# Storing the second-to-last row tile of an RMSNorm-matmul kernel by column chunk

## Chip, cores, metric

The kernel runs on 1 core of one Trainium2 chip. The metric is the device time in microseconds (us) of one execution. "Span" is the time from the first to the last instruction in a profile; the timed run of the same execution is 1.8 us longer in the kernel before.

## The reference, cut to what matters

```python
# x: (8, 1024, 768) f32, gamma: ones(768), w_qkv: (768, 2304) f32
rms = np.sqrt(np.mean(x ** 2, axis=-1, keepdims=True) + eps)
x_norm = x / rms * gamma
return np.matmul(x_norm, w_qkv).astype(np.float32)
```

The kernel takes x as 8192 rows, that is 64 row tiles of 128, and makes 2304 columns for each: four chunks of 512 columns and one of 256.

## The kernel before

The weights are converted to bf16 once (with gamma in them) and stay in SBUF. For each row tile x is loaded, cast, transposed by DMA, and multiplied; the factor 1/rms is applied when PSUM is evicted. VectorE and ScalarE take the evictions in turn. A tile's output has three parts: columns 0 to 1023, 1024 to 2047, and 2048 to 2303.

```python
# cut; the comments are added here
PARTS = [(0, 1024), (1024, 1024), (2048, N - 2048)]
...
outp = ctx.enter_context(tc.tile_pool(name="outp", bufs=7))
...
def store(t, h, n0, nl):
    p0 = PARTS[h][0]
    nc.sync.dma_start(out=of[t * P:(t + 1) * P, n0:n0 + nl], in_=OUT[t, h][:, n0 - p0:n0 - p0 + nl])
...
def evac_at(time, t, n0, eng, gap):
    at(time, evac, t, n0, eng)
    h = part(n0)
    nl = min(NT, N - n0)
    left[t, h] = left.get((t, h), PARTS[h][1]) - nl
    if t == MT - 1:                                   # last tile: a store for each chunk
        at(time + gap - 0.5, store, t, h, n0, nl)
    elif left[t, h] == 0:                             # others: a store for each part
        at(time + gap, store, t, h, *PARTS[h])
```

`at` only puts operations in an order; the times in it are the author's plan. All loads, transposes and stores are issued by SyncE, in that order.

Of the kernel before, what the change touches and what calls it, by code (L numbers as in the profile page):

```python
# [89 lines left out]
def kernel(  # L90
# [21 lines left out]
    MT = M // P  # L112
# [119 lines left out]
    def part(n0):  # L232
        return max(i for i, (p0, _) in enumerate(PARTS) if p0 <= n0)
# [21 lines left out]
    def at(time, fn, *args):  # L255
        plan.append((time, len(plan), fn, args))
# [8 lines left out]
    def evac_at(time, t, n0, eng, gap):  # L265
        at(time, evac, t, n0, eng)
        h = part(n0)
        nl = min(NT, N - n0)
        left[t, h] = left.get((t, h), PARTS[h][1]) - nl
        if t == MT - 1:  # L270
            at(time + gap - 0.5, store, t, h, n0, nl)
        elif left[t, h] == 0:
            at(time + gap, store, t, h, *PARTS[h])
# [13 lines left out]
    for time, op, *args in HEAD_PLAN:  # L287
        if op == "evac":

            evac_at(time, *args, gap=max(1.0, LOADS[-1][0] + 0.1 - time))  # L290
        elif op[-1] in "AB":
            at(time, tr_half if op[:2] == "tr" else cp_half, args[0], op[-1], *args[1:])
        else:
            if op == "mm":
                args[2] = [int(k) for k in args[2]]
            at(time, ops[op], *args)
# [4 lines left out]
    for t in range(HEAD, MT):  # L301

        ahead = 6.0 if t < HEAD + 5 else 0.0
        if ("x", t) not in {q[1:] for q in LOADS}:
            at(now - 15 - ahead, load_x, t)
        at(now - 8.5 - ahead, cast, t)
        at(now - 7.5 - ahead, xbar, t)
        at(now - 5, stat, t)
        at(now - 3, recip, t)
        for n0 in range(0, N, NT):  # L310
            at(now, mm, t, n0, range(KO))
            now += min(NT, N - n0) * US
            flip ^= 1
            evac_at(now + 0.2, t, n0, "DVE" if flip else "ACT", gap=1.2)
# [38 lines left out]
```

## Time and profile before

| | before |
|---|---|
| time, 3 runs | 389.31 us median (389.13 to 389.34) |
| span of the profiled run | 387.4 us |
| TensorE busy | 381.7 us, 99% |
| main matmuls in the chain that ended last | 94% of the span, without a break from 20.1 to 383.4 us |
| last store: issue, landing | 383.95 us, 2.0 us later |
| from the last issue to the end of the span | 3.44 us |

Some words for the end of the program. A store has "landed" when its completion semaphore has reached its full count, so that a waiting engine may go on. The DMAs use eight such semaphores in turn, the "lanes". At the close of the program SyncE makes five "closing checks", each of which waits for two semaphores, then a "drain", and then all engines meet in a barrier. "The step" is a gap of 0.39 us between the starts of two of these checks that no wait explains. A "record" is one line of SyncE's list in the trace.

Where this document gives times to three digits, they are taken from the instruction and DMA records of the trace.

### The profile page before, as it was taken

Reading aid. Unit: us, or ns where it says so; the run is one execution under the profiler, and the core shown is the slowest. Engines: PE = TensorE matmul, PEld = TensorE weight load, DVE = VectorE, ACT = ScalarE, POOL = GpSimd, SP = SyncE. Lnnn points to the kernel's source line nnn. Section 1 sums busy time; section 2 is a strip of 40 time slices with the busy share of each in tenths; the row PEclk is TensorE's granted clock in tenths of the full one; section 3 lists DMA queues with packets and bytes.
Section 4 is the critical chain, followed back from the end, with each engine's and each line's share of the span. In section 5 each row is a group of like instructions: output and inputs, shape, how many; then the busy total and the mean of one; then the engine's idle time right before and its main releaser. Section 6 shows DMA issues by size and latency. Waiting matters only on the chain.

```text
span 387.4 us, 5550 instructions
## 1 busy us (share of the span) xinstructions
PE 381.7 (99%) x1994; PEld 195.0 (50%) x1994; DVE 153.7 (40%) x309; ACT 181.2 (47%) x362; POOL 7.5 (2%) x15
## 2 busy tenths in 40 slices
PE   8999999999999999999999999999999999999995
PEld 7444654554554554554554554554554554554552
DVE  3565524434333344333344333344333343333331
ACT  5762444443544443544444544444444544444531
POOL 1312000000000000000000000000000000000000
PEclk9999999999999999999999999999999999999999
DMA  8999999999999999999999999999999999999975
GB/s 291 387 270 396 331 357 351 370 361 330 294 299 310 312 293 311 300 305 309 305 299 308 301 306 306 305 302 313 282 319 313 291 309 289 318 310 294 292 251 190
DMA packets 89223, 119.91 MB, mean 310 GB/s; under 512 B 52326, under 2 KB 61292, under 8 KB 89196
## 3 DMA queue, kind: packets, MB, share of 16 engines
q1 hardware_dynamic: 89184, 119.56, 101.1%
q8 instruction: 15, 0.25, 0.3%
q14 instruction: 12, 0.10, 0.1%
q10 hardware_dynamic: 12, 0.00, 0.0%
HBM read 32.25 MB, written 75.50 MB: 278 GB/s over the span
## 4 chain that ended last, share of the span: by engine, by line
PE 94%; DMA 4%; SPq 0%; DVE 0%; ACT 0%; issue 0%
PE pm L229 94%; DMA w_f<-in_w_qkv_dram 4%; SPq L153 0%; DVE w_b L164 0%; ACT ot L245 0%; SPq L158 0%
## 5 line engine op out<-in xcount | busy, mean ns | idle before, releaser
L229 PE MATMUL pm<-w_b,xT 128*128 128x512 bf16 (+1 forms) x1920 | 373.9, 358 | 0.6 <-DVE w_b L164 0.6
L229 PEld LDWEIGHTS <-xT 128*128 128x128 bf16 x1920 | 187.7, 98 | 186.1 <-issue 0.8
L243 DVE TENSOR_SCALAR ot<-pm,rstd 128x512 f32<-128x512 f32 (+1 forms) x165 | 113.6, 693 | 201.0 <-PE pm L229 200.7
L245 ACT ACTIVATE ot<-pm,rstd 128x512 f32<-128x512 f32 (+1 forms) x155 | 100.2, 648 | 190.6 <-PE pm L229 143.9
L183 ACT ACTIVATE sq<-x_t 128x768 bf16<-128x768 f32 x64 | 53.4, 834 | 2.0 <-DMA x_t<-in_x_dram 2.0
L172 DVE CAST xb<-x_t 128x768 bf16<-128x768 f32 x61 | 33.2, 544 | 18.2 <-DMA x_t<-in_x_dram 18.2
L185 ACT ACTIVATE rms<-ssq,eps_sb 128x1 f32<-128x1 f32 x64 | 18.9, 295 | 2.1
L183 ACT ACTIVATION_READ_ACCUMULATOR sq<-x_t 128x1 f32 x64 | 12.3, 192 | 0.0
L190 DVE RECIPROCAL rstd<-rms 128x1 f32<-128x1 f32 x64 | 9.8, 153 | 3.2 <-ACT rms L185 3.2
L166 ACT ACTIVATE w_b<-w_f,g_sb 128x512 bf16<-128x512 f32 (+1 forms) x9 | 5.8, 669 | 6.0 <-DMA w_f<-in_w_qkv_dram 6.0
L168 POOL TENSOR_SCALAR w_b<-w_f,g_sb 128x512 bf16<-128x512 f32 (+1 forms) x9 | 6.8, 765 | 24.3 <-DMA w_f<-in_w_qkv_dram 16.2
L164 DVE TENSOR_SCALAR w_b<-w_f,g_sb 128x512 bf16<-128x512 f32 (+1 forms) x12 | 5.2, 449 | 3.9 <-DMA w_f<-in_w_qkv_dram 3.9
L278 PE MATMUL pm<-warm 128*128 128x128 bf16 x49 | 5.4, 301 | 1.0 <-DVE eps_sb L137 1.0
L278 PEld LDWEIGHTS <-warm 128*128 128x128 bf16 x49 | 4.9, 142 | 1.0 <-DVE eps_sb L137 1.0
L210 PE MATMUL pm<-ident_f,x_t 128*128 128x128 f32 x18 | 2.5, 278 | 0.1
L210 PEld LDWEIGHTS pm<-ident_f,x_t 128*128 128x128 f32 x18 | 1.9, 141 | 0.5 <-DMA x_t<-in_x_dram 0.3
L172 DVE CAST xT<-pm 128x512 bf16<-128x512 f32 (+1 forms) x3 | 1.8, 592 | 0.5 <-PE pm L210 0.5
L140 ACT ACT_TABLE_LOAD x1 | 1.3, 1283 | 1.3 <-PEq L334 1.3
L174 ACT CAST xT<-pm 128x256 bf16<-128x256 f32 (+1 forms) x3 | 1.2, 445 | 0.3 <-PE pm L210 0.2
L174 ACT COPY xT<-pm 128x768 bf16<-128x768 bf16 x1 | 0.8, 799 | 0.3 <-PE pm L196 0.3
L261 DVE COPY g_sb<-pm 128x6 f32<-128x6 f32 x1 | 0.2, 165 | 1.8 <-PE pm L260 1.8
L196 PEld LDWEIGHTS <-xb 128*128 128x128 bf16 x6 | 0.4, 98 | 0.2
(13 smaller groups left out, 2.4 us busy)
## 6 DMA issues: line engine op xcount, KB each, us to landing
out_dram<-ot SPq DMA_DIRECT2D x126, 512.0 KB, 4.0
x_t<-in_x_dram SPq DMA_DIRECT2D x64, 384.0 KB, 4.3
out_dram<-ot SPq DMA_DIRECT2D x64, 128.0 KB, 3.3
w_f<-in_w_qkv_dram SPq DMA_DIRECT2D x7, 768.0 KB, 7.7
w_f<-in_w_qkv_dram SPq DMA_DIRECT2D x4, 256.0 KB, 5.9
out_dram<-ot SPq DMA_DIRECT2D x4, 256.0 KB, 2.0
xT<-xb SPq DMA_TRANSPOSE x60, 4.5
w_f<-in_w_qkv_dram SPq DMA_DIRECT2D x1, 512.0 KB, 4.2
```

The source lines that it names most:

```text
L164: nc.vector.tensor_scalar(out=o, in0=i, scalar1=g, scalar2=None, op0=mult)
L166: nc.scalar.activation(out=o, in_=i, func=AF.Copy, scale=g, bias=0.0)
L168: nc.gpsimd.tensor_scalar(out=o, in0=i, scalar1=g, scalar2=1.0, op0=mult, op1=mult)
L172: nc.vector.tensor_copy(out=out, in_=in_)
L183: nc.scalar.activation(out=sq, in_=X[t], func=AF.Square, accum_out=ssq)
L185: nc.scalar.activation(out=rms, in_=ssq, func=AF.Sqrt, scale=inv_k, bias=eps_sb)
L190: nc.vector.reciprocal(out=r, in_=RS[t])
L210: nc.tensor.transpose(out=PT[t, h][:, ko - k0, :], in_=X[t][:, ko * P:(ko + 1) * P], identity=ident_f)
L229: nc.tensor.matmul(out=PM[t, n0][:, :nl], lhsT=XT[t][:, ko, :], rhs=w_b[:, ko, n0:n0 + nl], start=(b == 1), stop=(b == KO))
L243: nc.vector.tensor_scalar(out=o, in0=pm[:, :nl], scalar1=RS[t], scalar2=None, op0=mult)
L245: nc.scalar.activation(out=o, in_=pm[:, :nl], func=AF.Copy, scale=RS[t], bias=0.0)
L278: nc.tensor.matmul(out=wps, lhsT=warm, rhs=warm, start=True, stop=True)
```

## The change

Since the last tile is already stored chunk by chunk, so that its data leaves as early as it can, the same is done for the tile before it. The intent is to have fewer bytes under way when the last stores begin.

```diff
-        if t == MT - 1:
+        if t >= MT - 2:
             at(time + gap - 0.5, store, t, h, n0, nl)
```

For this tile, stores of 512, 512 and 128 KB become four of 256 KB and one of 128 KB.

## The prediction

> **What bounds the kernel now.** I read the page first, then the chain of waits in order of time, and then, because the change touches only the second-to-last of 64 row tiles, the last 15 us of the trace. The page:
>
> ```profile
> PE 381.7 (99%) x1994; PEld 195.0 (50%) x1994; DVE 153.7 (40%) x309; ACT 181.2 (47%) x362; POOL 7.5 (2%) x15
> PE 94%; DMA 4%; SPq 0%; DVE 0%; ACT 0%; issue 0%
> L229 PE MATMUL pm<-w_b,xT 128*128 128x512 bf16 (+1 forms) x1920 | 373.9, 358 | 0.6 <-DVE w_b L164 0.6
> ```
>
> TensorE is busy for 99% of the span, the chain that ended last is 94% main matmuls, and those 1920 recorded matmuls waited 0.6 us in all. The engine is never held up by an output buffer or a store. The chain of waits in order of time ends like this:
>
> ```profile
> 20.12 363.25 PE pm L229 x1872
> 383.38 0.02 issue
> 383.40 0.47 ACT ot L245
> ```
>
> From 20.12 to 383.37 us it is one unbroken run of matmuls. Only what follows 383.4 us is not matmul: the last eviction (to 383.87), the last store and the closing of the program (to 387.4). So a change of stores can alter the time in two ways only: it disturbs the matmuls, or it moves something in the last 4 us.
>
> **The tail, before.** The timeline of ScalarE, VectorE and the store queue, asked in short windows (start, duration):
>
> ```profile
> 374.32 0.69 ACT L245 ACTIVATE ot<-pm,rstd 128x512 f32<-128x512 f32 x1 [0.97 <-PE pm L229]
> 375.04 0.33 SPq L249 DMA_DIRECT2D out_dram<-ot  x1
> 376.91 0.69 ACT L245 ACTIVATE ot<-pm,rstd 128x512 f32<-128x512 f32 x1 [1.90 <-PE pm L229]
> 377.63 0.33 SPq L249 DMA_DIRECT2D out_dram<-ot  x1
> 378.08 0.35 SPq L249 DMA_DIRECT2D out_dram<-ot  x1
> 383.40 0.47 ACT L245 ACTIVATE ot<-pm,rstd 128x256 f32<-128x256 f32 x1 [1.26 <-PE pm L229]
> 383.95 0.38 SPq L249 DMA_DIRECT2D out_dram<-ot  x1
> ```
>
> The three issues at 375.04, 377.63 and 378.08 are the present stores of the tile in question; each follows the eviction of the last chunk in its part by about 0.03 us (374.32 + 0.69 = 375.01). The issue at 383.95 is the last store of the last tile. The DMA engines in half-microsecond stretches (after the stretch: the engines' busy times and counts, then granted clock, DMA share, GB/s):
>
> ```profile
> 375.00:375.50 0.50, 0.50 (x4) 0.27 (x3) 0.00 (x0) 0.01 (x1) 0.00 (x0) 1.00 0.00 0
> 380.00:380.50 0.50, 0.50 (x4) 0.25 (x3) 0.34 (x1) 0.00 (x0) 0.00 (x0) 1.00 0.51 184
> 382.50:383.00 0.50, 0.50 (x6) 0.41 (x5) 0.25 (x1) 0.00 (x0) 0.00 (x0) 1.00 0.03 8
> 384.50:385.00 0.50, 0.00 (x0) 0.00 (x0) 0.00 (x0) 0.00 (x0) 0.00 (x0) 1.00 1.02 385
> 386.00:386.50 0.50, 0.00 (x0) 0.00 (x0) 0.00 (x0) 0.00 (x0) 0.00 (x0) 1.00 0.00 0
> ```
>
> There are holes in the transfers around 375, around 380.2 and again just before 383. Nothing of the second-to-last tile is still queued when the last stores start. After the last issue, the closing wait on SyncE and the landing times in this stretch are:
>
> ```profile
> L348 SPq EVENT_SEMAPHORE  x1: 1562/1562/1562, 384.4 to 384.4; - x1
> out_dram<-ot SPq DMA_DIRECT2D x4, 256.0 KB, 2.0
> ```
>
> So the end is: eviction done 383.87, issue 383.95, all landed 384.39 + 1.56 = 385.95 (2.0 us after the issue), a row of further semaphore checks and a barrier among the engines to 387.4, 1.45 us. The timed run of this profile was 389.19 us, 1.8 us above its span.
>
> **What the Trainium skill says.** "DMA: Bandwidth & Descriptors", section "Anatomy of one DMA", puts a fixed cost of about 2.0 us on a DMA, mostly the receipt of the last byte, plus bytes over 436 GB/s; that fit is for DMAs issued by GpSimd. The trace agrees in kind, with less: a 256 KB store lands in 2.0 us where the formula gives 2.6, a 512 KB store in 2.6 where it gives 3.2. The slope is the same 0.6 us for 256 KB. The fixed part therefore is a latency, which lies beside matmuls for every store except the last. The same page, "Rules for kernel authors", advises 1 MiB or more per DMA for bandwidth; splitting goes against that, but in the tail the 256 KB stores already move at a DMA share of 1.0 with some 385 GB/s, and half the stretches have room. "Perfetto Trace Analysis", section "Per-instruction lifecycle", says that the record of a DMA instruction leaves out the movement of the data; the trace agrees: 0.33 us of issue against 2.0 us to landing. I therefore count the 0.33 us as SyncE's cost and take the movement from the stretches.
>
> **The change part by part.** For the second-to-last tile, whose evictions end at 373.78, 375.01, 376.37, 377.60 and 378.05 (starts plus durations of the timeline), the order of the built program shows that three stores (512, 512, 128 KB) become five (four of 256 KB, one of 128). PE is unchanged; VectorE and ScalarE have the same work in the same order. Only SyncE's list is different.
>
> Removed: the two stores of 512 KB issued at 375.04 and 377.63. Added: four of 256 KB which I expect at 373.81, 375.04, 376.40 and 377.63, by the same 0.03 us after the eviction; the store of 128 KB stays at 378.08. Bytes are equal. SyncE pays 2 more issues of 0.33 us and 2 more semaphore checks with gaps, about 2 x 0.43 = 0.86 us (0.43 is the distance between back-to-back issues, 383.53 to 383.95). All of it falls between 373.8 and 376.8, where the queue has only waits: on the path, 0. The data: 256 KB take 0.65 us at 400 GB/s, and arrive every 1.3 us, so the first half of each part is gone before the second is evicted. The tile's last byte lands perhaps 0.3 us earlier than now (its last two transfers carry 384 KB in place of 640 KB). Nobody waits for it: the last tile's five stores are released by its own evictions, and the final 256 + 128 KB begin after a hole at 382.5 to 383.0. Gain from it: 0.
>
> One by-product remains. Completion semaphores rotate over eight lanes, and two more stores shift the last five by two lanes. In the built program the closing checks on SyncE each take two lanes in a fixed order. Before, the very first check holds the lane of the last store, so four more checks and a drain come after the landing (records at 386.00, 386.07, 386.14, 386.53, then 386.62). After the change the first check holds the store before the last, the second one the last store. So one check slips under the wait: about 0.07 us less. The step from 386.14 to 386.53 has 0.36 us of idleness that no wait explains; the end of SyncE's list also moves, so if this comes from its position there it may be hidden as well. Sum: 0.07 certain enough, up to 0.43 if both, so 389.31 - 0.1 = 389.2 us.
>
> **The rivals.** (1) A new wait takes the place of none: a store has to wait until the DMA eight earlier in the lanes has landed. With ten stores at the end, the last store waits for the second store of the changed tile, issued at about 375.04, landed by 377.1, needed at 383.9: 6.8 us to spare. The tightest others are the last tile's first stores, which wait for DMAs issued before 372.4 and landed by some 375, over 4 us before their turn. If I misread this, one store would be late by a microsecond: 390.3. Nothing speaks for it.
> (2) SyncE becomes the bound at the end: two issues push all later ones by 0.86 us, giving 390.2. Against it: between 378.44 and 379.58 the queue is idle, and each later store starts 0.03 us after its eviction.
> (3) The tail gains a microsecond, because the large stores held back the last tile: 388.3. Against it: all four 256 KB stores of the last tile land in 2.0 us already, the first too, and only the last landing counts.
> (4) The finer stores disturb the matmuls through memory traffic. Evictions follow at 1.29 to 1.30 us (six matmuls) at 368.5 to 376.9, whether the DMA share is 1.0 or 0. So 0.
>
> **Range and chances.** The three runs before lie within 389.13 to 389.34. A rebuilt program and another chip may move all by 0.1%, 0.4 us, which is more than any effect that I found. Point 389.2; range 388.7 to 389.6. A change of 2% is 7.8 us, more than the whole 4 us outside the matmuls, so within 2% at 0.99, the rest split evenly.
>
> **What would show it.** In the profile after: PE still at 99% with the chain's run of matmuls ending near 383.4; store issues near 373.8, 375.0, 376.4, 377.6, 378.1, and then the same five as before; 2.0 us to landing; the 1562 ns check gone or shorter, the wait for the last store now in the second check, and a span of 387.0 to 387.4. Wrong would be: the last issue later than 0.1 us after the last eviction, DMA busy at 383, a wait at the closing checks past 386.0, or a matmul run that is longer by over 0.3 us.

## The result

The changed kernel took 389.13 us (median of 6 runs, 388.87 to 389.33) against 389.32 us (6 runs, 389.08 to 389.57) before. The ratio is 0.9995, with a 95% interval of 0.9982 to 1.0008: the same. A ratio here is the mean time of one kernel's fast runs over that of the other's of the same rounds, so it is not quite the ratio of the medians.

The page of the changed kernel, the lines that answer to those of before:

```profile
PE 381.7 (99%) x1994; PEld 194.7 (50%) x1994; DVE 153.9 (40%) x309; ACT 181.2 (47%) x362; POOL 7.5 (2%) x15
PE 94%; DMA 4%; POOL 0%; SPq 0%; ACT 0%; issue 0%
L229 PE MATMUL pm<-w_b,xT 128*128 128x512 bf16 (+1 forms) x1920 | 374.1, 358 | 0.5 <-DVE w_b L164 0.4
```

TensorE has the same 381.7 us, the chain is again 94% matmuls, and they waited 0.5 us in all. The end of the chain in order of time:

```profile
17.94 365.63 PE pm L229 x1883
383.56 0.03 issue
383.59 0.47 ACT ot L245
```

The run of matmuls ends at 383.56 in place of 383.37 us. Its length counts from another point at the head (17.94 or 20.12 us), which comes and goes between executions of the changed kernel: a second profile of the changed kernel begins it at 20.04 and ends it at 383.29. This is noise of the start, about 0.2 us either way. The store queue in the timeline, four of the tile's issues and then the last issue of all:

```profile
373.99 0.33 SPq L249 DMA_DIRECT2D out_dram<-ot  x1
375.22 0.33 SPq L249 DMA_DIRECT2D out_dram<-ot  x1
376.58 0.33 SPq L249 DMA_DIRECT2D out_dram<-ot  x1
377.81 0.33 SPq L249 DMA_DIRECT2D out_dram<-ot  x1
...
384.15 0.37 SPq L249 DMA_DIRECT2D out_dram<-ot  x1
```

With 0.19 us taken off for the later matmuls these are the predicted 373.8, 375.0, 376.4 and 377.6. The last eviction ended at 384.06 and its store was issued at 384.15: the store queue is not late. The DMA engines by stretch (the last two columns are their busy share and GB/s):

```profile
380.00:380.50 0.50, 0.50 (x4) 0.22 (x3) 0.15 (x1) 0.00 (x0) 0.00 (x0) 1.00 0.00 0
382.60:383.10 0.50, 0.50 (x6) 0.35 (x5) 0.17 (x1) 0.00 (x0) 0.00 (x0) 1.00 0.12 41
384.50:385.00 0.50, 0.00 (x0) 0.00 (x0) 0.00 (x0) 0.00 (x0) 0.00 (x0) 1.00 0.90 336
```

The hole near 380 has become wider, so the tile's bytes do leave earlier: by the DMA records nothing moves from 379.86 to 380.60, before from 380.28 to 380.41 only. The hole before the last stores was there already and has moved with the matmuls (382.78 to 383.18, before 382.59 to 383.00; this is why the second stretch shown begins 0.1 us later than that of the prediction, which would have 0.30). The first two closing checks of SyncE (duration in ns, then start):

```profile
L348 SPq EVENT_SEMAPHORE  x1: 28/28/28, 385.8 to 385.8; - x1
L348 SPq EVENT_SEMAPHORE  x1: 28/28/28, 386.3 to 386.3; - x1
```

The record of 1562 ns is gone; the check that follows the last landing is now the second. In the kernel before, the step lay between the fourth and the fifth check:

```profile
L348 SPq EVENT_SEMAPHORE  x1: 28/28/28, 386.1 to 386.1; - x1
L348 SPq EVENT_SEMAPHORE  x1: 28/28/28, 386.5 to 386.5; - x1
```

In the changed kernel no two of the checks after the landing lie so far apart (0.07 us each). From the last issue to the end of the span there are 3.19 us in place of 3.44, in the second profile 3.07. So the tail is 0.25 to 0.37 us shorter. This small gain is what the experiments had to explain: do the earlier bytes make it, or only the two stores more in SyncE's list, which move the closing checks?

### The profile page after: what moved, and what is told of

It reads as the page before. It is cut to its first block, busy times and chain, and to the rows that moved or that the text cites. A ratio compares the mean times of both kernels' runs of the same rounds, so it can differ in the third digit from the quotient of the medians.

```text
span 387.3 us, 5554 instructions
## 1 busy us (share of the span) xinstructions
PE 381.7 (99%) x1994; PEld 194.7 (50%) x1994; DVE 153.9 (40%) x309; ACT 181.2 (47%) x362; POOL 7.5 (2%) x15
## 4 chain that ended last, share of the span: by engine, by line
PE 94%; DMA 4%; POOL 0%; SPq 0%; ACT 0%; issue 0%
PE pm L229 94%; DMA w_f<-in_w_qkv_dram 3%; DMA x_t<-in_x_dram 1%; POOL w_b L168 0%; ACT ot L245 0%; SPq L158 0%; SPq L153 0%
```

## The experiments

The theory: the tile's stores lie beside the matmuls and are worth nothing, and what little is gained comes from having two stores more in SyncE's list before the closing. Three groups follow: what the closing does, what the tile's stores can cost, and what is the same in other tiles. Each edit is against the kernel before.

### The kernel before, profiled again (no edit)

> The kernel before, unchanged, profiled a second time. In its first profile the closing of the program has a step of 0.39 us between the starts of the fourth and the fifth semaphore check (386.14 to 386.53) that no wait explains; in the changed kernel's profile it is gone. Theory fixed step: it belongs to the program and comes again, 0.35 to 0.40 us, between the same two checks. Rival chance: it was a single event of that execution, and the fifth check now follows the fourth by about 0.07 us. Both: last matmul run ends within 0.3 us of 383.4, the last store lands 2.0 us after its issue.

One run, 389.23 us. The step came again: fourth check at 386.195, fifth at 386.583, 0.388 us apart, of which 0.360 us no record fills. From the last issue to the end 3.43 us. So it belongs to the program.

### The same shift without touching the tile

```diff
-        if t == MT - 1:
+        if t in (30, MT - 1):
```

> Tile 30 is stored in five stores in place of the second-to-last tile, which keeps its three. Same number of stores, same shift of completion lanes and the same length of SyncE's list as in the changed kernel, but the tail's stores are as before. Theory by-product: whatever the changed kernel gains at the end comes from the shift alone, so from the last issue to the end of the span there are 3.2 us here as in the changed kernel (before: 3.44), with no step of 0.36 us in the closing checks. Rival finer stores: the gain came from the tile's own stores, and the closing takes 3.44 us here. Total in both cases within 0.3 us of 389.2.

389.07 us against 389.52 of before on the same chip, ratio 0.9986 (0.9971 to 1.0001). From the last issue to the end 3.035 us, with no step in the checks. The second of them waits for the last landing, and the drain follows the fifth at 386.46.

```profile
L348 SPq EVENT_SEMAPHORE  x5: 28/28/28, 385.8 to 386.4; - x5
```

The second-to-last tile has its three old stores here, and the tail is as short as in the changed kernel, or shorter. The finer stores of that tile are not what shortens it.

### One store more

```diff
+        elif left[t, h] == 0 and h == 0 and t in (30,):
+            at(time + gap, store, t, h, 0, 512)
+            at(time + gap, store, t, h, 512, 512)
         elif left[t, h] == 0:
```

> Tail as in the kernel before; one 512 KB store of tile 30 cut in two, so one store more in all, the last store in completion lane 3 (the first closing check still waits for it), SyncE's list two instructions longer. For the unexplained step of 0.36 us three theories. Place in the list: the step sits at one fixed place of SyncE's instruction list, so it moves to the third closing check, and from the landing of the last store to the closing drain it takes some 0.67 us as before. Branch: it comes five instructions after the branch into the closing block, so it is at the fifth check again, also 0.67 us. Waiting in execution: it follows a check that waits for its second semaphore while executing, as in the kernel before (record of 1.56 us); here the last store is the first semaphore of the first check, so no step, and 0.31 us from landing to drain. Total within 0.3 us of 389.3.

One run, 389.39 us. The closing checks of this kernel (its closing line is L351), the first four:

```profile
L351 SPq EVENT_SEMAPHORE  x1: 28/28/28, 386.1 to 386.1; - x1
L351 SPq EVENT_SEMAPHORE  x1: 28/28/28, 386.2 to 386.2; - x1
L351 SPq EVENT_SEMAPHORE  x1: 27/27/27, 386.6 to 386.6; - x1
L351 SPq EVENT_SEMAPHORE  x1: 28/28/28, 386.7 to 386.7; - x1
```

The step is now between the second and the third check (386.213 to 386.601), two checks earlier, as the list is two instructions longer. From landing to drain 0.68 us. The branch theory (fifth check) and the theory of the wait in execution (no step) fall; the theory of place stands. The odd record of 1562 ns also has its rule: it appears where the last store's semaphore is the second of a check's two in the built program, and the record is 28 ns where it is the first, as here.

### Three stores more

The edit is the same with `t in (20, 25, 30)`.

> Tail as in the kernel before; three 512 KB stores in mid-kernel cut in two. The last store goes to completion lane 5, so the third closing check waits for it, and SyncE's list is six instructions longer. The unexplained step followed the place in SyncE's list so far (the fifth check before, the third with one store more, none seen with two). Theory place: here the place holds the issue of the last store itself, so the step of 0.36 us delays that issue: 0.45 to 0.55 us after the end of the last eviction in place of 0.08, and nothing hides it; from the last eviction to the end of the span 3.6 us (before 3.5). Rival: the step is a matter of the closing block alone; the issue follows the eviction by 0.08 us and no step appears. Total near 389.4 against 389.1.

One run, 389.43 us. The last eviction and the last issue in the timeline:

```profile
383.56 0.47 ACT L245 ACTIVATE ot<-pm,rstd 128x256 f32<-128x256 f32 x1 [1.26 <-PE pm L229]
384.45 0.33 SPq L249 DMA_DIRECT2D out_dram<-ot  x1
```

The eviction ends at 384.03 and the issue follows 0.43 us later; in all kernels of this tail without that step it follows by about 0.1 us. So the step can be moved onto the last store itself, and from the end of the eviction to the end of the span there are 3.61 us, as expected. The records show a regular place: SyncE's records 80, 208, 336, 464 and 592, counted from one, so 128 apart, have an idle time of 0.34 to 0.46 us before them in all fourteen traces, where adjacent records without a wait have some 0.05 us. The exception is a record that waits for other reasons as well, as record 592 of the changed kernel does (1.24 us), where the step cannot be told apart from the wait.

The traces also hold a hint of what happens there. The profile lists a DMA queue called "instruction", and from 376 us to the end the changed kernel has one packet of 8 KB on it:

```profile
q14 instruction: 1, 0.01, 0.2%
```

By the DMA records it begins at 385.70, 1.18 us after record 591 ended. In the other traces too an 8 KB packet follows 1.0 to 1.5 us after the end of record 591, wherever that lies between 381 and 390 us. In the kernel with chunks in all tiles record 591 ends at 281.5 us, the packet follows 2.6 us later, and there is none in the last 20 us of the span. So SyncE most likely fetches instructions at these places. Where the step can be seen it is over before the packet begins, so it is not a wait for this packet; what it consists of stays open.

### Five stores more, twice

The edit is the same with `t in (20, 25, 30, 35, 40)`.

> Tail as in the kernel before; five 512 KB stores of tiles 20 to 40 cut in two, which puts the last store in completion lane 7, so that the fifth and last closing check waits for it and the other four lie under its landing. Theory lanes: from landing to the closing drain about 0.1 us, where the kernel before has 0.67 and the changed kernel 0.27 or a little more; from the last issue to the end of the span 2.85 to 3.0 us (before 3.44, changed 3.2). Rival no effect of the lanes: 0.3 us or more from landing to drain. Total 388.8, that is 0.5 us less than before, which three rounds can hardly tell from the noise of 0.2 us; the trace decides.

> The kernel of split5 again, with more rounds, beside the changed kernel on the same chip. Theory: from the last issue to the end of the span 2.8 us again (before 3.44, changed 3.19), total 0.5 to 0.6 us under the kernel before, 388.7 to 389.0, ratio 0.9985. Rival noise: the same total as before within 0.2 us.

388.94 us against 389.52, ratio 0.9984 (0.9968 to 1.0001), and on another chip 388.84 against 389.50, ratio 0.9983 (0.9969 to 0.9998). The last issue and some closing checks of the first of the two:

```profile
384.09 0.38 SPq L249 DMA_DIRECT2D out_dram<-ot  x1
```

```profile
L351 SPq EVENT_SEMAPHORE  x1: 28/28/28, 384.5 to 384.5; - x1
...
L351 SPq EVENT_SEMAPHORE  x1: 28/28/28, 386.1 to 386.1; - x1
```

The first check is done at 384.5 and the last, which waits for the last store, begins at 386.06; the drain follows at 386.13. From the last issue to the end 2.79 us in both profiles, a little less than the expected 2.85 to 3.0. That is 0.64 us less than before and 0.28 to 0.40 less than in the changed kernel, without a change in the tail's own stores. This is the fastest kernel, though at 0.17% still "the same".

### The changed kernel again (no edit)

> The changed kernel again, with more rounds. Theory by-product: from the last issue to the end of the span 3.03 to 3.2 us, no step in the closing checks, total 0.2 to 0.4 us under the kernel before, ratio 0.9990 to 0.9995. Rival finer stores matter: 1 us or more less. Rival noise: ratio 1.0000 with both signs among the rounds.

389.06 us against 389.50, ratio 0.9987 (0.9971 to 1.0002). From the last issue to the end 3.07 us, no step. The medians lie 0.44 us apart, a little more than expected, but the interval still includes 1, so by the clock alone a gain is not shown; this trace shows 0.37 us, the first one 0.25.

### The tile in 36 stores

```diff
-        if t == MT - 1:
-            at(time + gap - 0.5, store, t, h, n0, nl)
+        if t >= MT - 2:
+            step = 64 if t == MT - 2 else nl
+            for c in range(n0, n0 + nl, step):
+                at(time + gap - 0.5, store, t, h, c, step)
```

> The second-to-last tile in 36 stores of 64 columns in place of 5. Theory issue cost: SyncE is a queue that needs 0.43 to 0.45 us for one store with its check; 36 of them from 373.8 us take until 389.5, and the five of the last tile follow, so the last issue comes at 391.3 in place of 383.95 and the total is 7.0 to 7.5 us longer, 396.5, slower by 1.8 to 1.9%, with the matmul run ending at 383.4 as before. Rival transfers: the small rows make the DMA engines the bound, so that landings take far over 2 us and the total is longer still. Rival hidden anyway: no change.

398.66 us, ratio 1.0234 (1.0218 to 1.0251): slower. The last eviction, which ends the chain of matmuls, and the last issue:

```profile
383.43 0.47 ACT ot L245
```

```profile
393.02 0.52 SPq L249 DMA_DIRECT2D out_dram<-ot  x1
```

The matmuls end as ever, and the store queue works on for 9 us. The mechanism is the expected one, issue cost on SyncE; its size was put too low. In this queue a small store takes 0.475 us, not 0.43 to 0.45, and one step (record 592) falls into it as well. The small stores land in 1.5 us (median), so the DMA engines are not the bound, and the rival of slow transfers falls. For the five larger stores that come last within 2 us, landing took up to 2.7 us.

### The tile in 18 stores

The same edit with `step = 128`.

> The second-to-last tile in 18 stores of 128 columns. Theory issue cost, with the 0.48 us for one small store that the run with 36 stores showed: 18 x 0.48 = 8.6 us from 373.8 end at 382.4, the last tile's stores catch up at 0.43 us each, and the last issue comes at 384.0 to 384.3, at most 0.3 us late; the lane shift (last store in the second closing check) gives 0.3 us back, so 389.2 to 389.5 in total. So 15 stores more cost nothing, 33 more cost 9 us. Rival proportional cost: each store added costs the same, 9.2 us / 33 x 15 = 4.2 us.

390.19 us against 389.46, ratio 1.0019 (1.0000 to 1.0038), some 0.7 us longer, where 389.2 to 389.5 was expected. The last issue is at 384.55 us, 0.67 us after the end of its eviction at 383.87, and I had expected at most 0.3. In the records the last tile's stores catch up at 0.47 to 0.50 us each rather than 0.43, and record 592, with 0.36 us of idleness before it, falls among the small stores before them. Back to back, the last stores land in up to 2.6 us. Still, 15 stores more for the tile cost 0.7 us and 33 more cost 9: cost in proportion (4.2 us) is refuted. Up to about this number there is room in the queue.

### The tile's three stores held back to the end

```diff
         if t == MT - 1:
+            if n0 + nl == N:
+                for k, part_ in enumerate(PARTS):
+                    at(time + gap - 0.6, store, t - 1, k, *part_)
             at(time + gap - 0.5, store, t, h, n0, nl)
-        elif left[t, h] == 0:
+        elif left[t, h] == 0 and t != MT - 2:
```

> The three stores of the second-to-last tile are held back until just before the last store: the same bytes and as many stores as before, but now in front of the last store. Theory: a transfer of this tile costs only where it stands ahead of the last store in the DMA queues. Three issues of 0.43 us put the last issue 1.3 us later, and 256 + 512 + 512 + 128 + 128 KB from 384.3 at 400 GB/s end at 388.3, so the last landing is near 388.7 in place of 385.95 and the total 2.5 to 3 us longer, 391.8 to 392.3. Rival, bandwidth of the tail does not matter: 1.3 us longer by the issues alone, 390.6.

391.96 us against 389.46, ratio 1.0064 (1.0047 to 1.0081), 2.5 us longer. The DMA engines by stretch and the issues:

```profile
385.00:386.00 1.00, 0.00 (x0) 0.00 (x0) 0.00 (x0) 0.00 (x0) 0.00 (x0) 1.00 1.01 406
386.00:387.00 1.00, 0.00 (x0) 0.00 (x0) 0.00 (x0) 0.00 (x0) 0.00 (x0) 1.00 1.01 401
```

```profile
384.81 0.97 SPq L249 DMA_DIRECT2D out_dram<-ot  x1
385.88 1.13 SPq L249 DMA_DIRECT2D out_dram<-ot  x1
```

Here the engines move the 1536 KB without a break from 384.28 to 388.47, and the first closing check ends at 388.85, where 388.7 was expected for the landing. The last two issues take 0.97 and 1.13 us in place of some 0.35, and the last comes some 2 us late; why is not settled. Since the engines never pause, the row of bytes sets the end and not the late issue. This shows what the change could have been good for: bytes of this tile cost time where they stand in front of the last store. In the kernel before they do not.

### The last tile in three stores

```diff
-        if t == MT - 1:
+        if t == MT:
```

> The last tile too is stored in three stores in place of five. Theory: what column chunks are worth they are worth in the last tile alone. The 512 KB of its second part start after the eviction at 383.5, in place of 256 KB, so the last landing is 256 KB / 400 GB/s = 0.65 us later; two stores less put the last store in completion lane 0, third closing check, which gives 0.14 us back, and the step of 0.36 us in the list moves past the checks or not. Total 0.1 to 0.7 us longer than before, 389.6 to 390.1. Rival: the fixed time to landing hides the size and nothing changes.

389.63 us against 389.46, ratio 1.0003 (0.9987 to 1.0018). The time to landing of the last two stores:

```profile
DMA to landing us min/median/max: 2.6/2.6/2.6
```

The last landing is 0.6 us later, as estimated. From the last issue to the end 3.72 us, only 0.28 more than before: the last store is waited for in the third check and the step has moved past the checks, so that from landing to drain there are 0.20 us in place of 0.67, and the step gives 0.16 us of this back in the barrier that follows. So chunks are worth 0.6 us at the last landing, in the last tile. The clock alone does not tell the two kernels apart.

### Chunks in all tiles

```diff
-        if t == MT - 1:
+        if t >= HEAD:
```

> All tiles from the seventh on are stored by column chunk, five stores in place of three, 114 issues more in all. Theory: stores lie beside the matmuls all along, SyncE needs 5 x 0.43 + 1.3 (transpose) + 0.4 (load) = 3.9 us of a tile's 5.8 us, so no wait appears and the total is within 0.4 us of 389.2. Rival traffic: finer stores disturb matmuls or delay the loads and transposes behind them in SyncE's list, and the matmul run gets holes: over 390.

390.06 us (389.32 to 390.57) against 389.46, ratio 1.0017 (0.9998 to 1.0036), which is not clear of noise. The expectation of 389.2 within 0.4 was missed by the median. The one profiled execution was the fastest of the four, and its matmuls waited 0.6 us in all and ended at 383.62, so it shows no cost. The other executions had spans of 387.9 to 388.5 and no profile: whether something was lost there, and where, stays open. About half of the 0.6 us by which the median exceeds that of the kernel before lies outside the span: in all four executions the timed run is 2.1 us longer than the span, before 1.8. The interval's upper end bounds it at 0.4%.

## Why the prediction was right

**The bound.** The step "one unbroken run of matmuls" held. The matmuls of the main line waited 0.6 us before and 0.5 us after in all, and the run ends between 383.3 and 383.7 us in the kernels whose ends were read, even where the store queue is 9 us behind.

**The issues.** The 0.86 us of extra SyncE work lay in idle time, as the issue times show; the last store still follows its eviction by 0.09 us. The price of 0.43 us for an issue was right for single stores. In a row it was 0.475 us, so the term of the sum was low by a tenth. This had no weight in the changed kernel and gave wrong sizes in the two runs with many stores.

**The data.** "Gain from it: 0" was right. Its side estimate, that the tile's last byte lands 0.3 us earlier, was low: 380.20 in place of 380.63, and 0.62 us earlier when the later matmuls are taken off. The "hole around 380.2" that the prediction read was in truth only 0.13 us long before the change, but the last tile's first store was not held back by it: its bytes move 0.83 us after its issue, as those of the next one do. The hole grew, and nobody waited for what was gained there. The held-back run shows that it would have counted if those bytes had stood before the last store.

**The by-product.** The prediction gave 0.07 us for the check that slips under the wait, and up to 0.43 us if the unexplained step depended on its place in the list. It does: one, three and five stores more moved it as its place says. From the start of the second check to the drain there were 0.62 us before and 0.27 us after, so 0.35 us of the 0.43 came true inside the checks. In the first profile of the changed kernel the last store took 0.12 us longer to be seen as landed (2.17 us from issue to the second check, 2.05 in the kernel before), which leaves 0.23 of the 0.25 us seen there; the rest lies behind the drain. In one detail the prediction misread the list: the fourth and fifth check hold one lane each, beside a semaphore that is none of the eight. The checks that its argument needs do hold two.

**The signs.** Two of the marks that I had named for "wrong" were met by the letter. The matmul run was longer by over 0.3 us (365.63 in place of 363.25), but only because it counts from another point at the head; its end moved by 0.19 us. And the second check began at 386.3, past 386.0. It was no new wait. The matmuls ended 0.19 us later in that execution, and the landing took the said 0.12 us more; in the second profile the same check began at 385.92. The latter mark should have been a distance from the last issue, not a time of the clock.

**The rivals.** No lane wait held a store. SyncE as the bound would have been 390.2; it takes some 15 stores more, not 2, before it costs 0.7 us. A gain of a microsecond did not come. Finer stores did not disturb the matmuls in any profile, including the one with 114 more issues.

The predicted 389.2 lies within 0.1 us of the measured 389.13, though that is closer than the noise allows one to claim: it is in part luck, since the point took 0.1 us for an effect that the traces show as 0.25 to 0.37.

## What to carry to other kernels

In this kernel, splitting a store could pay only where its bytes stand in front of the store that ends the program; look for holes in the DMA stretches before the last issue, and where there is one, leave the earlier stores alone. For a change in the last 4 us, measure from the last issue to the end of the span, because differences of 0.3 us were here lost in the noise of the clock. When such a difference appears, first run a control that shifts the instruction list by the same amount elsewhere: here it gave all of the gain.

## What the Trainium skill lacked or had wrong

- "Runtime: NRT & Kernel Launch", section "Instruction fetch mechanics": it says that a queue is refilled in blocks of 256 instructions and that crossing a boundary is mostly hidden. SyncE's records 80, 208, 336, 464 and 592 have 0.34 to 0.46 us of idleness before them. So the spacing on SyncE is 128, half of the page's figure, and the packets on the "instruction" queue that follow have 8 KB. It shows wherever no other wait covers it, and once it delayed the last store by 0.36 us. That the refill is the cause is an inference from the spacing and from these packets; no experiment separates it.
- "Perfetto Trace Analysis", section "Per-instruction lifecycle": it says that the record of a sequencer-only instruction leaves the semaphore wait out. Here a semaphore check is 1562 ns long when it waits on the second of two semaphores (1954, 1793 and 2023 ns in three other kernels), and 28 ns when it waits on the first.
- "DMA: Bandwidth & Descriptors", section "Anatomy of one DMA": its fit, 2.0 us plus bytes over 436 GB/s, is for DMAs issued by GpSimd; for DMAs issued by SyncE it has no such fit. For stores issued by SyncE the traces have 2.0 us for 256 KB and 1.5 us for 32 KB, so about 0.6 us less than the fit.
- The pages that I read give no cost for one store on SyncE of this chip: 0.33 us recorded, 0.43 us from one issue to the next, 0.475 us in a long row of small stores.
- The pages that I read do not say that the order of the closing checks can be worth time: from the last issue to the end of the span there were 3.44 us where the last store was waited for in the first check and 2.79 us where it was in the fifth, some 0.3 us of it through the step named above.
